# Up projections of two MLPs by Strassen's seven block products, with the residual and the hidden activations kept in DRAM

## The chip, the cores and the metric

The kernel runs on one core of a Trainium2 chip. The metric is device time in microseconds (us) of one execution. The kernel before takes 3135.95 us, the median of three runs (3134.9 to 3142.02).

## The reference

A two-layer trunk is run for two request groups that share the weights: 1024 new tokens of one stream (prompts) and 16 tokens of each of 8 running streams (samples), 1152 tokens in all, width 1024, all float32. The first layer mixes tokens by forgetting attention beside causal pooling, the second by stick-breaking attention. Behind each mixer stands an MLP, and each sub-layer is normalized, shifted and scaled by a conditioning vector, and added to the residual through a gate (w_up is 1024 x 4096, w_down 4096 x 1024):

```python
def _sq_relu_mlp(h, w_up, w_down):
    return jnp.square(jax.nn.relu(h @ w_up)) @ w_down
...
h = _rmsnorm(x, norm_g[i, 1]) * (1 + sc2) + sh2
x = x + g2 * _sq_relu_mlp(h, w_up[i], w_down[i])
```

## The kernel before

**Layout.** The residual is held transposed in SBUF, as `xT[c]`: three chunks c of 384 tokens, each with 8 blocks (`k`) of 128 channels on the partitions. Chunk 2 holds the last 256 prompt tokens and the 128 sample tokens. `h`, the normalized input, is a pair of such tiles per chunk.

**Numbers in two parts.** Every float32 operand of TensorE (PE) is a pair: a high part of type fp32r, made by a cast, and a low part, value minus high part. A product is three matmuls for each k: high by high, high by low, low by high (`lin_chunk`, L480 to L489, its matmul in L486). `split` (L181 to L187) makes the pair of a weight: the cast on ScalarE (ACT, L184), the low part on GpSimd (POOL, L185).

**An MLP.** `mlp` (L496 to L546) calls `norm` (L506), whose `norm_chunk` applies scale and shift: prompts by VectorE (DVE, L437), ACT (L440, L446), and a low part on DVE (L447) or POOL (L442); samples by L455 to L461. The sums of squares are added in L351. `up` (L509 to L524) takes one block f of 128 hidden channels, loads its weights (`load_cols`, 512 KB on the queue of SyncE, SP), and for each chunk issues 24 matmuls of 384 columns; then ACT takes the relu from PSUM (L520), DVE squares (L521), ACT casts the high part (L522) and DVE makes the low part (L523). `down` (L526 to L536) takes two such blocks, loads their rows of w_down (`load_rows`, L217), and for each chunk and each output block n issues 6 matmuls and adds the gated result to `xT` (`x_add`, L469 to L478: L472 on DVE, and for chunk 2 also L476 on DVE and L478 on POOL). The loop in L538 to L546 alternates up of one pair and down of the pair before, so hidden activations never leave SBUF.

**Order.** A scheduler orders each engine's instructions by their priority, which is the order of the code unless it is set: `at(i)` gives the norm of chunk i the priority of a place in the last down (or in the mixer's last output projection), where `pin` and `before` fix the norm's small matmuls between given output blocks (`PIN_M`, `PIN_O`). `tick` (called in up and down) issues part of the small matmuls that work out the next conditioning vectors (`ada_group`). Loads go through SP's queue, stores through ACT's.

## Time and profile before

| | |
|---|---|
| median of 3 runs | 3135.95 us (3134.9 to 3142.02) |
| the profiled execution | 3139.25 us |
| its span in the trace | 3137.4 us |
| mean granted clock of PE | 0.991 |
| busy share of the span | PE 98%, DVE 52%, ACT 33%, POOL 27% |
| moved by DMA | 330.93 MB, mean 105 GB/s |

Durations come from the one profiled execution; its time is 3.3 us above the median, and 1.85 us of it lie outside the span. An engine's busy time counts its computing instructions only. A granted clock of 1.00 is the full one. In a timeline "x3" joins three like instructions in a row, and the bracket behind a row gives the idle time ahead of it and what ended that.

### The profile page before, as it was taken

How to read it: one execution, taken by the hardware profiler on the slowest of the kernel's cores; microseconds unless marked ns; L12 is line 12 of the kernel's file. 1: busy time of each engine (PE TensorE's matmuls, PEld its weight loads, DVE VectorE, ACT ScalarE, POOL GpSimd, SP SyncE). 2: the span in 40 equal slices, each digit the busy share in tenths (PEclk: the TensorE clock that was granted, in tenths of full speed). 3: DMA queues.
4: the chain of work that ended last, by engine and by line, in shares of the span. 5: the costliest groups of instructions: out<-in, count | busy, mean ns of one | idle time of the engine just before them, and what ended most of it. 6: DMA issues, size and time to landing. Idle time of an engine off the chain costs nothing.

```text
span 3137.4 us, 51121 instructions
## 1 busy us (share of the span) xinstructions
PE 3066.5 (98%) x20558; PEld 2815.7 (90%) x20558; DVE 1637.3 (52%) x3204; ACT 1036.8 (33%) x2222; POOL 852.0 (27%) x759
## 2 busy tenths in 40 slices
PE   7999999999999999999999999999999999999998
PEld 5888868789999999999999967777789999999998
DVE  5234767674444444446300078888874444444546
ACT  5322334441212121213422276666651211212122
POOL 3212111052222222223411133443352222222222
PEclk9999999999999999999999999999999999999999
DMA  7677443312232321111555563544301111111111
GB/s 267 202 217 239 149 138 106 104 50 88 88 101 82 93 74 40 43 41 34 177 177 169 179 219 117 177 126 139 106 28 42 46 41 41 47 35 48 34 48 68
DMA packets 333617, 330.93 MB, mean 105 GB/s; under 512 B 33820, under 2 KB 292548, under 8 KB 333381
## 3 DMA queue, kind: packets, MB, share of 16 engines
q1 hardware_dynamic: 257041, 261.27, 26.9%
q10 hardware_dynamic: 76340, 66.39, 6.4%
q8 instruction: 163, 2.67, 0.4%
q14 instruction: 73, 0.60, 0.1%
HBM read 256.51 MB, written 71.09 MB: 104 GB/s over the span
## 4 chain that ended last, share of the span: by engine, by line
PE 89%; DVE 5%; DMA 2%; ACT 1%; issue 1%; POOL 1%; SPq 0%; ACTq 0%; DVEq 0%; POOLq 0%
PE ps_s L486 38%; PE ps_a L486 18%; PE ps_t L486 16%; PE ps_a L987 4%; PE ps_t L967 3%; PE ps_m L232 2%; PE ps_s L951 2%; DVE sn L905 1%; PE ps_s L952 1%; PE ps_s L1046 1%; PE ps_m L1034 1%; PE ps_t L1071 1%; DVE sg L908 1%; PE ps_s L954 1%; PE ps_t L618 0%
## 5 line engine op out<-in xcount | busy, mean ns | idle before, releaser
L185 POOL TENSOR_TENSOR w_lo<-w_raw,w_hi 128x1024 fp32r<-128x1024 f32 (+1 forms) x184 | 441.5, 2402 | 994.8 <-ACT w_hi L184 947.4
L486 PE MATMUL ps_s<-h,w_hi 128*128 128x384 f32 x2080 | 541.2, 339 | 8.1 <-DVE h L447 4.8
L184 ACT CAST w_hi<-w_raw 128x1024 fp32r<-128x1024 f32 (+1 forms) x184 | 190.4, 1049 | 935.7 <-PE ps_t L486 364.0
L472 DVE SCALAR_TENSOR_TENSOR xT<-ps_s,modT,xT 128x384 f32<-128x384 f32 (+1 forms) x516 | 294.2, 571 | 244.1 <-PE ps_s L486 242.4
L486 PEld LDWEIGHTS ps_s<-h,w_hi 128*128 128x128 f32 x2080 | 379.8, 189 | 14.9 <-DVE h L447 6.6
L478 POOL TENSOR_TENSOR xT<-xT,xs 128x128 f32<-128x128 f32 x320 | 155.8, 487 | 739.2 <-DVE xs L476 732.7
L486 PE MATMUL ps_s<-h,w_lo 128*128 128x384 f32 x1040 | 353.1, 340 | 0.0
L486 PE MATMUL ps_s<-oh,w_hi 128*128 128x384 f32 x792 | 269.1, 340 | 0.0
L486 PE MATMUL ps_s<-oh,w_lo 128*128 128x384 f32 x792 | 266.9, 337 | 0.0
L486 PE MATMUL ps_s<-ol,w_hi 128*128 128x384 f32 x792 | 266.3, 336 | 0.0
L486 PE MATMUL ps_a<-h,w_hi 128*128 128x384 f32 x944 | 244.1, 339 | 0.0
L905 DVE TENSOR_TENSOR_SCAN sn<-sn 128x128 f32<-128x128 f32 (+4 forms) x224 | 218.0, 1002 | 43.9 <-ACT sn L899 39.0
L486 PE MATMUL ps_t<-h,w_hi 128*128 128x384 f32 x816 | 210.4, 339 | 0.0
L908 POOL TENSOR_TENSOR sg<-sg,sn 128x512 f32<-128x512 f32 (+3 forms) x112 | 136.9, 1222 | 257.8 <-DVE sn L905 195.0
L523 DVE TENSOR_TENSOR ol<-r,oh 128x384 fp32r<-128x384 f32 x192 | 158.9, 829 | 86.0 <-ACT oh L522 85.5
L486 PEld LDWEIGHTS ps_s<-h,w_lo 128*128 128x128 f32 x1040 | 196.7, 189 | 0.1
L521 DVE SCALAR_TENSOR_TENSOR r<-ps_s,r 128x384 f32<-128x384 f32 x102 | 56.7, 556 | 261.2 <-ACT r L520 261.2
L472 DVE SCALAR_TENSOR_TENSOR xT<-ps_a,modT,xT 128x256 f32<-128x256 f32 (+1 forms) x252 | 143.7, 570 | 84.3 <-PE ps_a L486 83.7
L486 PEld LDWEIGHTS ps_a<-h,w_hi 128*128 128x128 f32 x944 | 171.2, 188 | 7.0 <-issue 6.7
L973 ACT COPY pt<-ps_t 128x512 f32<-128x512 f32 (+3 forms) x256 | 125.9, 498 | 128.2 <-PE ps_t L967 126.6
L486 PE MATMUL ps_s<-w_hi,h 128*128 128x256 f32 (+1 forms) x800 | 157.9, 286 | 4.4 <-ACT h L446 4.4
L486 PE MATMUL ps_a<-h,w_lo 128*128 128x384 f32 x472 | 159.8, 338 | 0.0
(306 smaller groups left out, 6849.0 us busy)
## 6 DMA issues: line engine op xcount, KB each, us to landing
w_raw<-in_w_ada_dram SPq DMA_DIRECT2D x80, 512.0 KB, 4.1
w_raw<-in_w_up_dram SPq DMA_DIRECT2D x64, 512.0 KB, 4.2
w_raw<-in_w_down_dram SPq DMA_DIRECT2D x64, 512.0 KB, 3.3
Q<-q SPq DMA_DIRECT2D x100, 256.0 KB, 3.8
q<-qt ACTq DMA_DIRECT2D x48, 384.0 KB, 5.5
vr<-in_cache_sb_v_dram SPq DMA_DIRECT2D x32, 512.0 KB, 4.9
kr<-in_cache_sb_k_dram SPq DMA_DIRECT2D x32, 512.0 KB, 4.0
out_dram<-kv ACTq DMA_DIRECT2D x48, 256.0 KB, 2.9
```

The costliest lines, as they stand in the source:

```text
L184: after(nc.scalar.copy(hi[:, :n], raw[:, :n]), "act")
L185: after(nc.gpsimd.tensor_tensor(lo[:, :n], raw[:, :n], hi[:, :n].bitcast(F32), op=ALU.subtract), "pool")
L232: nc.tensor.matmul(acc[32 * j:32 * j + 32, :], lhsT=condT[:, k, :], rhs=raws[j // 2][:, j % 2 * 512:(j % 2 + 1) * 512], start=(k == 0), st ...
L472: nc.vector.scalar_tensor_tensor(xT[c][:, n, :npc], ps[:, :npc], g[:, n, 0:1], xT[c][:, n, :npc], op0=ALU.mult, op1=ALU.add)
L478: nc.gpsimd.tensor_tensor(xT[c][:, n, 256:], xT[c][:, n, 256:], t, op=ALU.add)
L486: mm = nc.tensor.matmul(ps, lhsT=a, rhs=b, start=(i == 0), stop=(i == n - 1))
L523: nc.vector.tensor_tensor(ol[:, c], r, oh[:, c].bitcast(F32), op=ALU.subtract)
L905: nc.vector.tensor_tensor_scan(rev, rev, rev, initial=1.0, op0=ALU.mult, op1=ALU.bypass)
L908: eng.tensor_tensor(sg[:, 0:m - 1], sg[:, 0:m - 1], sn[:, 1:m], op=ALU.mult)
L967: nc.tensor.transpose(T[:, kb * P:(kb + 1) * P], pr[:, kb * P:(kb + 1) * P], ident)
L973: nc.scalar.copy(pt.rearrange("p k n -> p (k n)")[:, 0:n], T[:, 0:n])
L987: nc.tensor.matmul(A[rs, os_], lhsT=Vd[kb // 4][:, kb % 4, rs], rhs=PTs[h2][kb], start=(kb == 0), stop=(kb == i))
```

## The change

The MLP becomes two phases, `up_phase` and `down_phase`, and only up changes its arithmetic.

- **Up by seven products.** Two blocks f form a pair g, 16 pairs in all. The weights of a pair are a 2 x 2 of blocks (two halves of 512 input channels, two blocks f), and the input of a token half (`tp`, 576 of the 1152 tokens) is a 2 x 2 of blocks of 512 channels by 288 tokens. Their product takes seven block products (Strassen, in Winograd's form) in place of eight. Each is 12 matmuls of 288 columns: 4 k by three pairs of parts.
- **Forms of the input.** Seven forms of a token half (`forms`: blocks 11, 21, 22 and the sums T1 to T4) are made from the normalized input by subtractions on DVE (`sub`) and each split in two parts (`parts`): the cast on ACT, the low part on POOL for two in three and on DVE for the third. The norm is applied in place, in `X`, which is now one tile.
- **Forms of the weights.** For each pair four loads of 256 KB (`raw_block`) and four sums on DVE, and each of seven forms is split by `w_parts`, on ACT and POOL.
- **Putting together.** Products are added in PSUM where they can be, and with DVE where not (`add`, `finish`); P2's square is taken from PSUM. Freed columns of `X` serve as scratch (`slot`).
- **Passes.** Pairs 0 to 2 are done on the first token half alone, then pairs 0 to 2 on the second, then 3 to 14 on both with one set of weights, then 15 on the second and on the first. `late` spreads the norm of the rest and the forms of the second half over the first three passes.
- **DRAM.** The residual is stored chunk by chunk behind the mixer's last output projection (on SP) and read back in `down_phase`; hidden activations are stored by up (on ACT's queue, 144 KB each) and read back in rows of 1152 tokens, and split there.
- **Down** takes four blocks f at a time (12 matmuls between two `x_add` calls), the first time with the chunks in the order 2, 1, 0.

The core of the diff; its last lines are those of the mixer's output projection.

```diff
-A1 = 0.25
+A1 = 0.3
...
-PIN_M = (4, 11)
+PIN_M = (2, 6)
+TB = 288
+UR = 6
+UW = 4
+UG = 3
+DR = 4
+HB = 6
...
-    xT = [const.tile([P, KD, CW], F32, name=f"xT{c}") for c in range(NCH)]
+    X = const.tile([P, KD, T_ALL], F32, name="xT")
+    xT = [X[:, :, c * CW:(c + 1) * CW] for c in range(NCH)]
+    x_sc = [dram.tile([P, KD, CW], F32, name=f"x{c}") for c in range(NCH)]
+    hid_sc = [dram.tile([2, P, T_ALL], F32, name=f"hid{g}") for g in range(FF // P // 2)]
...
+    def up_phase(l):
...
+        w = w_up[l]
+        forms = ("11", "21", "T2", "T1", "T3", "22", "T4")
...
+            def apply(c, sd, k, c0, c1):
+                x = xT[c][:, k, c0:c1]
+                nc.vector.scalar_tensor_tensor(x, x, A[:, k, 0:1], sd[:, c0:c1], op0=ALU.mult, op1=ALU.mult)
+                nc.scalar.activation(x, x, AF.Identity, bias=B[:, k, 0:1])
...
+            def parts(form, tp, j, src):
+                hi, lo = (t[:, j, :] for t in F[form][tp])
+                rr["f"] = rr.get("f", 0) + 1
+                nc.scalar.copy(hi, src)
+                (nc.vector if rr["f"] % 3 == 0 else nc.gpsimd).tensor_tensor(lo, src, hi.bitcast(F32), op=ALU.subtract)
...
+            def sub(o, a, b):
+                nc.vector.tensor_tensor(o, a, b, op=ALU.subtract)
+            def other_forms(tp, j):
+                b11, b12, b21, b22 = (blk(tp, j, r, c) for r in (1, 2) for c in (1, 2))
+                parts("22", tp, j, b22)
+                sub(b11, b12, b11)
+                sub(b12, b22, b12)
+                sub(b22, b22, b11)
+                parts("T2", tp, j, b22)
+                parts("T1", tp, j, b11)
+                parts("T3", tp, j, b12)
+                sub(b21, b21, b22)
+                parts("T4", tp, j, b21)
...
+            KO = (0, 4, 1, 5, 2, 6, 3, 7)
+            with at(0):
+                sd = rstd_of(0, np_, 0)
+                for i, k in enumerate(KO):
+                    apply(0, sd, k, 0, TB)
+                    if i % 2:
+                        first_forms(0, i // 2)
+                for k in KO:
+                    apply(0, sd, k, TB, CW)
+            with at(1):
+                sd1 = rstd_of(1, np_, 1)
+                h1 = 2 * TB - CW
+                for i, k in enumerate(KO):
+                    apply(1, sd1, k, 0, h1)
+                    if i % 2:
+                        other_forms(0, i // 2)
+            pins.clear()
+            def late():
...
+                for k in KO:
+                    apply(1, sd1, k, h1, CW)
+                yield
+                sd = rstd_of(2, np_, 2)
+                yield
+                for i, k in enumerate(KO):
+                    apply(2, sd, k, 0, 256)
+                    if i % 2 == 0:
+                        samples(sd, i // 2 * 2, i // 2 * 2 + 2)
+                    if i % 2:
+                        yield
+                for j in range(4):
+                    first_forms(1, j)
+                    yield
+                for j in range(4):
+                    other_forms(1, j)
+                    yield
...
+            def raw_block(g, r, c):
+                t = ur.tile([P, 4, P], F32, name="u_raw", tag="raw", bufs=UR)
+                f = 2 * g + r - 1
+                nc.sync.dma_start(t, w[(c - 1) * 512:c * 512, f * P:(f + 1) * P].rearrange("(k p) n -> p k n", p=P))
...
+            def w_parts(src):
+                hi = uw.tile([P, 4, P], F32R, name="u_hi", tag="hi")
+                lo = uw.tile([P, 4, P], F32R, name="u_lo", tag="lo")
+                nc.scalar.copy(hi, src)
+                nc.gpsimd.tensor_tensor(lo, src, hi.bitcast(F32), op=ALU.subtract)
+                return hi, lo
...
+                def form(self, f):
+                    a = self.a
+                    if f == "P6":
+                        sub(a[2, 1], a[1, 1], a[2, 1])
+                        s2 = ur.tile([P, 4, P], F32, name="u_raw", tag="raw", bufs=UR)
+                        sub(s2, a[2, 2], a[2, 1])
+                        a["s2"] = s2
+                        return w_parts(s2)
+                    if f == "P5":
+                        nc.vector.tensor_tensor(a[1, 1], a["s2"], a[1, 1], op=ALU.add)
+                    if f == "P3":
+                        sub(a[1, 2], a[1, 2], a["s2"])
+                    return w_parts(a[{"P1": (1, 1), "P2": (1, 2), "P5": (1, 1), "P7": (2, 1), "P3": (1, 2), "P4": (2, 2)}[f]])
...
+            FORM = {"P1": "11", "P2": "21", "P6": "T2", "P5": "T1", "P7": "T3", "P3": "22", "P4": "T4"}
...
+            def product(p, ws, tp, ps, start):
+                wh, wl = ws
+                mh, ml = F[FORM[p]][tp]
+                i = 0
+                for k in range(4):
+                    for a, b in ((wh, mh), (wh, ml), (wl, mh)):
+                        mm = nc.tensor.matmul(ps, lhsT=a[:, k, :], rhs=b[:, k, :], start=(start and i == 0), stop=(i == 11), skip_group_check=not start)
...
+            def out(u, r, c, t):
+                tok = (2 * u["tp"] + c - 1) * TB
+                nc.scalar.dma_start(hid_sc[u["g"]][r - 1, :, tok:tok + TB], t)
...
+            def add(o, ps, b):
+                nc.vector.tensor_tensor(o, ps, b, op=ALU.add)
...
+            def finish(u, r, c, ps, b):
+                t = slot("h", 8, 8)
+                add(t, ps, b)
+                nc.vector.scalar_tensor_tensor(t, t, 0.0, t, op0=ALU.max, op1=ALU.mult)
+                out(u, r, c, t)
...
+                    if p == "P1":
+                        u["b1"] = ps_t()[:, :TB]
+                        product(p, ws, tp, u["b1"], True)
+                        u["p1"] = slot("p1", 0, 4)
+                        nc.scalar.copy(u["p1"], u["b1"])
+                    elif p == "P2":
+                        product(p, ws, tp, u["b1"], False)
+                        t = slot("h", 8, 8)
+                        nc.scalar.activation(t, u["b1"], AF.Relu)
+                        nc.vector.scalar_tensor_tensor(t, u["b1"], 0.0, t, op0=ALU.max, op1=ALU.mult)
+                        out(u, 1, 1, t)
+                    elif p == "P6":
+                        u["b2"] = ps_s()[:, :TB]
+                        product(p, ws, tp, u["b2"], True)
+                        u["u2"] = slot("u2", 4, 2)
+                        add(u["u2"], u["b2"], u["p1"])
+                    elif p == "P5":
+                        u["b3"] = (ps_a if tp else ps_s)()[:, :TB]
+                        product(p, ws, tp, u["b3"], True)
+                        u["p15"] = slot("p15", 6, 2)
+                        add(u["p15"], u["b3"], u["p1"])
+                    elif p == "P7":
+                        product(p, ws, tp, u["b2"], False)
+                        finish(u, 2, 2, u["b2"], u["p15"])
+                    elif p == "P3":
+                        product(p, ws, tp, u["b3"], False)
+                        finish(u, 1, 2, u["b3"], u["u2"])
+                    elif p == "P4":
+                        product(p, ws, tp, u["b2"], False)
+                        finish(u, 2, 1, u["b2"], u["p1"])
...
+            NG = FF // P // 2
+            passes = ([(g, (0,)) for g in range(UG)] + [(g, (1,)) for g in range(UG)]
+                      + [(g, (0, 1)) for g in range(UG, NG - 1)] + [(NG - 1, (1,)), (NG - 1, (0,))])
+            fill = late()
+            prev = None
+            for i, (g, tps) in enumerate(passes):
+                if i == UG:
+                    for _ in fill:
+                        pass
+                us, wts = [{"g": g, "tp": tp} for tp in tps], Weights(g)
+                for p in ("P1", "P4", "P2", "P6", "P5", "P7", "P3"):
+                    if p == "P4":
+                        if prev:
+                            stage(p, *prev)
+                    else:
+                        stage(p, us, wts)
+                    next(fill, None)
+                prev = us, wts
+            stage("P4", *prev)
+    def down_phase(l):
...
+            for c in (2, 1, 0):
+                for k in range(KD):
+                    nc.sync.dma_start(xT[c][:, k, :], x_sc[c][:, k, :])
+            NF = FF // P
+            for f0 in range(0, NF, DR):
+                last = f0 + DR == NF
+                if last and l == 0:
+                    have((1, 2))
                 ws, hs = [], []
...
+                for f in range(f0, f0 + DR):
+                    raw = hid.tile([P, NCH, CW], F32, name="hr", tag="hr", bufs=3)
+                    nc.sync.dma_start(raw.rearrange("p c n -> p (c n)"), hid_sc[f // 2][f % 2])
+                    ws.append(load_rows(w_down[l], f * P, wx if f % 2 else None))
+                    oh, ol = (hid.tile([P, NCH, CW], F32R, name=n, tag=n, bufs=HB) for n in ("oh", "ol"))
+                    nc.scalar.copy(oh, raw)
+                    nc.vector.tensor_tensor(ol, raw, oh.bitcast(F32), op=ALU.subtract)
+                    hs.append((oh, ol))
+                if last:
+                    order = [(c, n) for c in range(NCH) for n in range(KD)]
+                elif f0 == 0:
+                    order = [(c, n) for c in (2, 1, 0) for n in range(KD)]
+                else:
+                    order = [(c, n) for n in range(KD) for c in range(NCH)]
                 for c, n in order:
...
                         if last:
                             pin(c, n, mm, PIN_O)
+                            nc.sync.dma_start(x_sc[c][:, n, :], xT[c][:, n, :])
...
```

Three excerpts of the order of instructions follow. Line numbers in the second fence of each are those of the changed kernel.

First, POOL at the start of the MLP of layer 1, before: low parts of weights (L185), of the normalized chunks (L442), and the samples.

```order
L185 TENSOR_TENSOR w_lo<-w_raw,w_hi 128x1024
L478 TENSOR_TENSOR xT_74<-xT_74,xs 128x128
L442 TENSOR_TENSOR h_24206<-xa,h_24205 128x384
L351 TENSOR_TENSOR sb<-sb,nw 128x384
L442 TENSOR_TENSOR h_24206<-xa,h_24205 128x384 x3
L185 TENSOR_TENSOR w_lo<-w_raw,w_hi 128x1024
L442 TENSOR_TENSOR h_24208<-xa,h_24207 128x384 x4
```

POOL at the same place now: low parts of the forms of the first token half (L548, tiles F and FT) and of the first weight forms (L622).

```order
L548 TENSOR_TENSOR F_25027<-xT,F_25026 128x288 x2
L622 TENSOR_TENSOR u_lo<-u_raw,u_hi 128x512 x3
L548 TENSOR_TENSOR FT_25019<-xT,FT_25018 128x288
L548 TENSOR_TENSOR F_25027<-xT,F_25026 128x288
L548 TENSOR_TENSOR FT_25019<-xT,FT_25018 128x288
L548 TENSOR_TENSOR FT_25023<-xT,FT_25022 128x288 x2
L548 TENSOR_TENSOR FT_25015<-xT,FT_25014 128x288
L548 TENSOR_TENSOR FT_25019<-xT,FT_25018 128x288
L548 TENSOR_TENSOR FT_25023<-xT,FT_25022 128x288
L622 TENSOR_TENSOR u_lo<-u_raw,u_hi 128x512
```

Where 8 low parts of two chunks stood among two of weights, 19 low parts of the first half now stand among the weights' low parts, and as many of the second half follow.

Second, SP at the start of the MLP of layer 1, before: loads of w_up and w_down alone.

```order
L217 DMA w_raw<-in_w_down_dram 128x1024
L195 DMA w_raw<-in_w_up_dram 128x8x128 x2
L217 DMA w_raw<-in_w_down_dram 128x1024 x2
L195 DMA w_raw<-in_w_up_dram 128x8x128 x2
L217 DMA w_raw<-in_w_down_dram 128x1024 x2
```

SP now: loads of weight blocks (L615), and among them the reloads of chunk 2 of the residual (L746) into columns that the forms of the second half are made from.

```order
L615 DMA u_raw<-in_w_up_dram 128x4x128 x8
L746 DMA xT<-x_72 128x384
L615 DMA u_raw<-in_w_up_dram 128x4x128 x2
L746 DMA xT<-x_72 128x384 x2
L615 DMA u_raw<-in_w_up_dram 128x4x128
L746 DMA xT<-x_72 128x384 x4
L615 DMA u_raw<-in_w_up_dram 128x4x128
L746 DMA xT<-x_72 128x384
L615 DMA u_raw<-in_w_up_dram 128x4x128 x63
```

The eight reloads of chunk 2 came in ahead of the weights of the fourth pass; a reload waits for the last reader of its columns.

Third, ACT where the first operands of down are made in layer 0, before: casts of hidden activations (L522) stand right behind each relu (L520), among the norm's.

```order
L520 ACTIVATE r<-ps_s 128x384
L440 ACTIVATE xa<-xa,modT 128x256
L520 ACTIVATE r<-ps_s 128x384
L446 ACTIVATE h_7007<-xa,modT 128x256
L441 CAST h_7007<-xa 128x256
L522 CAST oh<-r 128x384
L460 CAST h_7007<-xs 128x3x128
L522 CAST oh<-r 128x384
```

ACT now, at the end of up: the last stores of hidden activations (L669), casts of w_down (L202), and the casts of the rows read back (L758).

```order
L669 DMA hid_88<-xT 128x288
L202 CAST w_hi<-w_raw 128x1024
L669 DMA hid_88<-xT 128x288
L758 CAST oh<-hr 128x1152 x3
L202 CAST w_hi<-w_raw 128x1024 x2
L758 CAST oh<-hr 128x1152 x3
L202 CAST w_hi<-w_raw 128x1024
```

Down's casts moved behind the last store of up, and take whole rows of 1152 tokens.

## Rows read from the trace of the kernel before

**Rows 1.** The page's first part: busy time, share of the span, instructions.
```profile
PE 3066.5 (98%) x20558; PEld 2815.7 (90%) x20558; DVE 1637.3 (52%) x3204; ACT 1036.8 (33%) x2222; POOL 852.0 (27%) x759
```

**Rows 2.** By stretch: from:to, us, busy PE, PEld, DVE, ACT, POOL, PEclk, DMA share, GB/s.
```profile
642.00:1490.00 848.00, 845.12 (x4846) 818.73 (x4847) 409.94 (x785) 192.33 (x331) 239.16 (x219) 1.00 0.22 68
2302.00:3123.00 821.00, 817.10 (x4674) 816.21 (x4673) 405.81 (x777) 187.50 (x321) 235.64 (x219) 1.00 0.14 42
```

**Rows 3.** The chain in order of time, in up of layer 1: start, us, link.
```profile
2373.37 4.22 PE ps_s L486 x24
2377.59 4.21 PE ps_t L486 x24
```

**Rows 4.** PE's timeline at the second mixer: start, us; the second is 24 matmuls later.
```profile
1590.35 0.28 PE L486 MATMUL ps_s<-w_hi,h 128*128 128x256 f32 x1
...
1593.17 0.28 PE L486 MATMUL ps_a<-w_hi,h 128*128 128x256 f32 x1
```

**Rows 5.** PE's timeline at the MLP start of layer 1, first, third and last of it.
```profile
2303.83 0.62 PE L486 MATMUL ps_s<-h,w_hi 128*128 128x384 f32 x2 [1.67 <-ACT h L446]
...
2306.69 0.69 PE L486 MATMUL ps_s<-h,w_hi 128*128 128x384 f32 x1 [2.23 <-DVE h L447]
...
2311.01 0.52 PE L486 MATMUL ps_s<-h,w_hi 128*128 128x384 f32 x1
```

**Rows 6.** By stretch: the MLP start of layer 1, and the busiest DMA.
```profile
2300.00:2310.00 10.00, 6.09 (x28) 5.58 (x28) 9.85 (x18) 5.85 (x12) 7.80 (x7) 0.74 0.17 53
1540.00:1560.00 20.00, 19.34 (x165) 19.14 (x164) 1.12 (x2) 3.91 (x11) 0.89 (x1) 1.00 0.83 264
```

**Rows 7.** POOL's timeline: two places where DVE waits beside it.
```profile
641.52 2.36 POOL L185 TENSOR_TENSOR w_lo<-w_raw,w_hi 128x1024 fp32r<-128x1024 f32 x1
...
2341.35 4.79 POOL L185 TENSOR_TENSOR w_lo<-w_raw,w_hi 128x1024 fp32r<-128x1024 f32 x2 [4.74 <-ACT w_hi L184]
```

**Rows 8.** DVE's timeline at the same places, and the MLP start of layer 1.
```profile
642.14 2.15 DVE L351 TENSOR_TENSOR sa<-sa,nw 128x384 f32<-128x384 f32 x1
...
2301.60 1.65 DVE L437 SCALAR_TENSOR_TENSOR xa<-xT,Ad,ps_a 128x384 f32<-128x384 f32 x3
...
2343.96 3.53 DVE L523 TENSOR_TENSOR ol<-r,oh 128x384 fp32r<-128x384 f32 x3
```

**Rows 9.** By line: ns of one at least, median, most; first to last start.
```profile
L523 DVE TENSOR_TENSOR ol<-r,oh x192: 545/559/2593, 660.0 to 3094.0; 128x384 fp32r<-128x384 f32 x192
...
L521 DVE SCALAR_TENSOR_TENSOR r<-ps_s,r x102: 543/558/560, 658.0 to 3092.9; 128x384 f32<-128x384 f32 x102
...
L437 DVE SCALAR_TENSOR_TENSOR xa<-xT,Ad,ps_a x96: 468/603/616, 43.0 to 2334.2; 128x384 f32<-128x384 f32 x64, 128x256 f32<-128x256 f32 x32
...
L442 POOL TENSOR_TENSOR h<-xa,h x48: 733/1017/1384, 45.8 to 2335.9; 128x384 fp32r<-128x384 f32 x32, 128x256 fp32r<-128x256 f32 x16
...
L773 POOL TENSOR_TENSOR pw<-w_raw,pw x1: 1290/1290/1290, 88.3 to 88.3; 128x512 fp32r<-128x512 f32 x1
...
L772 ACT CAST pw<-w_raw x1: 616/616/616, 85.8 to 85.8; 128x512 fp32r<-128x512 f32 x1
...
L459 POOL TENSOR_TENSOR xs<-xs,modT x12: 620/846/906, 75.4 to 2334.1; 128x384 f32<-128x384 f32 x8, 128x256 f32<-128x256 f32 x4
...
L659 ACTq DMA_DIRECT2D q<-qt x36: 520/521/906, 88.3 to 1813.2; - x36
```

**Rows 10.** DMA issues: KB each, median us from issue to landing.
```profile
w_raw<-in_w_up_dram SPq DMA_DIRECT2D x64, 512.0 KB, 4.2
w_raw<-in_w_down_dram SPq DMA_DIRECT2D x64, 512.0 KB, 3.3
```

More of the change, by code (lines that the diff above doesn't have):

```diff
@@ new lines, in up_phase @@
+            ur = es.enter_context(tc.tile_pool(name=f"ur{l}", bufs=1, side="right", reuse_waits="tile"))
+            uf = [es.enter_context(tc.tile_pool(name=f"uf{l}{tp}", bufs=1, reuse_waits="tile",
+                                                **({"side": "right"} if tp == 0 else {}))) for tp in range(2)]
+            uw = es.enter_context(tc.tile_pool(name=f"uw{l}", bufs=UW, side="right", reuse_waits="tile"))
+            F = {f: [[uf[tp].tile([P, 4, TB], F32R, name=f"F{f}{i}", tag=f"F{f}{i}") for i in range(2)] for tp in range(2)]
+                 for f in forms}
@@ new lines, in up_phase, with slot @@
+            FORM = {"P1": "11", "P2": "21", "P6": "T2", "P5": "T1", "P7": "T3", "P3": "22", "P4": "T4"}
+            last = {}
+            cnt = {}
+            def slot(kind, base, n):
+                i = cnt[kind] = cnt.get(kind, -1) + 1
+                i = base + i % n
+                return X[:, i % KD, i // KD * TB:(i // KD + 1) * TB]
+            def product(p, ws, tp, ps, start):
[5 more added lines that the diff above has]
+                        mm = nc.tensor.matmul(ps, lhsT=a[:, k, :], rhs=b[:, k, :], start=(start and i == 0), stop=(i == 11), skip_group_check=not start)
+                        if i == 0 and "mm" in last:
+                            behind(mm, last["mm"])
+                        i += 1
+                last["mm"] = mm
@@ L532, in down, with mlp, __init__ @@
                                    for (wh, wl), (oh, ol) in zip(ws, hs)])
-                    x_add(c, n, ps, g, mp)
-                    tick(0.25)
+                    x_add(c, n, ps, g, hid)
+                    tick(0.5)
                     if last:
                         pin(c, n, mm, PIN_M)
-            prev = (0, up(0, 1, order=M_ORD))
-            for f in range(2, FF // P, 2):
-                cur = up(f)
-                down(*prev, False)
-                cur += up(f + 1)
-                prev = (f, cur)
-            if l == 0:
-                have((1, 2))
-            down(*prev, True)
+    def mlp(l):
+        close_weights()
+        up_phase(l)
+        open_weights(f"wpool{l + 1}")
+        down_phase(l)
     class Npool:
         B = {"sa": 1, "sb": 1, "nw": 2, "xa": 3, "rc": 2}
-        def __init__(self, pool):
-            self.pool = pool
+        def __init__(self, pool, bufs=None):
+            self.pool, self.B = pool, bufs or self.B
         def tile(self, shape, dt, name, tag):
```

92 lines of the change are left out of this document (51 added, 41 removed).

## Prediction

> **What bounds the kernel now.** I read the page's first part, then a table by stage, then the timelines of single engines. TensorE (PE) is busy 98% of the span [rows 1], and in the two MLPs it is the only bound: 845.1 of 848 us and 817.1 of 821 us, at a granted clock of 1.00 [rows 2]. VectorE (DVE) and GpSimd (POOL) are busy about half and a quarter of the time there. So an MLP is worth its matmuls, and only PE columns saved, or PE made to wait, can move the end.
>
> A 384-column matmul starts every 4.215 / 24 = 175.6 ns [rows 3], and 24 matmuls of 256 columns take 2.82 us, 117.5 ns each [rows 4]. Both are 0.458 ns a column.
>
> The one weak place is the start of each MLP. PE idles 1.67 and 2.23 us, and the 13 matmuls behind that come 0.32 us apart, the 1.2 GHz level, granted clock 0.74 in that slice [rows 5, 6]. It loses 3.9 + 13 x (0.332 - 0.176) = 5.9 us in all, while ScalarE (ACT), DVE and POOL normalize and split the activations.
>
> The rows to remember are those of DVE beside POOL. A DVE operation whose two tensors both lie in SBUF stands still while a POOL operation runs: 0.55 us of work took 2.15 beside a POOL operation of 2.36, three took 3.53 behind the second of two, and they ended 1.35 us after it, 0.45 each [rows 7, 8]. L523 (two SBUF tensors) reads 545 at best and 2593 ns at worst; L521 and L437 (one of them in PSUM) never move [rows 9]. POOL waits for DVE in the same way: L442 goes from 1017 to 1384 ns [rows 9].
>
> **The gain.** Before, up is 32 x 3 x 24 = 2304 matmuls of 384 columns in a layer: 404.6 us. After, 16 pairs of f, two token halves, seven products of 12: 2688 of 288 columns. No row has 288; the bounds are 117.5 and 175.6 ns. I take 132.0, on the line between, since both ends have the same price per column; an end would need a step in it, so I keep 3% of doubt. 2688 x 132.0 = 354.8 us, **49.8 saved in a layer, 99.6 in both**. The Trainium skill (TensorE: Matmul & The Clock Gate, Back-to-back issue gap) gives N / 2.4 GHz + 2.5 ns, an estimate of 162.5 and 122.5 ns here, and 45.1 saved in a layer. The trace disagrees with its 162.5, so the rows stand; by the page the sum would be 9 us higher.
>
> Down has as many matmuls of the same width, at nothing. Its x_add calls halve, on a DVE that does not bound. The ada matmuls only change place.
>
> **What replaces it at the start.** Seven forms of each activation block, and of each weight block, must be made and split, and most of this is DVE work on two SBUF tensors or POOL work. By the rows above those two do not overlap, so I add them up. Prices [rows 9]: POOL 512 columns 1.29 us, 288 columns 0.80 (between 0.733 at 256 and 1.017 at 384), 384 columns 1.0; DVE, from the 0.45 at 384, 0.34 at 288 and 0.60 at 512.
>
> - Forms of one token half: 28 low parts, two thirds on POOL (19 x 0.80) and 9 x 0.34 on DVE, and 16 subtractions x 0.34: 23.7 us. Twice.
> - Norm of the third chunk: 3 x 1.0 + 4 x 0.45, and 8 POOL operations for the samples, at 0.62 (L459's least): 9.8.
> - Weights of the three passes ahead of the second half: 20 low parts x 1.29, 12 subtractions x 0.60, 8 finishes x 0.34: 35.7. In layer 0 four of each of the first two stand ahead of the start by the order: 28.1.
>
> Together 92.9 us in layer 1 and 85.3 in layer 0. In front stand 32 apply operations on DVE, 11.5 us by L437, beside which POOL finds about 4 us of work: 7.5 more. So the second half's forms are ready at T + 93 (layer 0) and T + 100 (layer 1), T being where DVE begins to apply the norm (2301.6 in layer 1, [rows 8]). Three passes on that half follow, each with 7 x 1.29 + 4 x 0.60 + 3 x 0.34 = 12.4 us of this work for 84 x 0.132 = 11.1 of PE: T + 130 and T + 137. PE has 6 x 11.1 = 66.5 us of work by then. It **loses 63.5 and 70.5 us, 57.6 and 64.6 more than now**. Passes on both halves need 13.4 us for 22.2 of PE, so from there PE bounds again.
>
> That rule is in the Trainium skill too (SBUF — State Buffer, Who interferes with whom): an exclusive lock for a whole instruction, for DVE with two SBUF inputs against a GpSimd read. The rows agree at 384 and 1024 columns; for 288 no run here shows it. Without it the sum is that of the first rival.
>
> ACT is no bound: a single pass costs it 7 x 0.62, two PSUM reads of about 0.5 and four store issues of 0.52 [rows 9], 7.4 us. Nor is DMA: 1.05 MB of weights and 0.59 MB of stores in 11.1 us are 148 GB/s, where 264 are seen [rows 6]; a mean of 100 in the other passes.
>
> **Three smaller waits**, each per layer. On SP four weight loads of the fourth pass stand behind reloads of x that wait for the second half's forms; a load lands in 4.2 us [rows 10], and two products of 1.6 us lie ahead: 0 to 6, I take 2. The last two passes are single again (12.4 for 11.1), with four weight buffers ahead: 0 to 3, take 1. Between up and down, the first hidden rows are read behind reloads that wait for the last stores, and ACT's splits of them stand behind the last store issue. One landing of about 4 us [rows 10] and an ACT and a DVE pass over 1152 columns: 3 to 13, take 6, as the weights are split by then.
>
> **Sum.** Layer 0: 57.6 + 9 - 49.8 = +16.8. Layer 1: 64.6 + 9 - 49.8 = +23.8. The profiled execution took 3139.25 us, so 3179.9; the median of the runs is 3.3 below it, so **3177 us**.
>
> **Rivals.** *Faster: the two engines overlap well enough that POOL alone sets the start.* Many of DVE's operations here are only 0.34 us and may slip in where POOL waits for ACT. POOL's own work is 38 x 0.80 + 8.0 + 16 (layer 1: 20) x 1.29 = 59 and 64 us, with the 7.5 in front T + 67 and T + 72; the next three passes run at PE's 11.1. PE loses 33.5 and 38.5, 27.6 and 32.6 more than now, plus 5 each: 33 + 38 - 100 = -29, so 3107. For it speaks that DVE has other work to do beside POOL; against it the rows, where even one operation waited POOL out. It decides from about 48 us lost at the start.
>
> *Slower still: the chain through PSUM.* P7, P3 and P4 add into a bank that DVE must read first, and that read is queued on DVE behind operations that wait for POOL. A POOL operation (1.29) for each of 18 such products in six single passes is 23 us a layer: 3223. In double passes another product lies between, so it is hidden there. PE at 1.2 GHz after each gap would add to it.
>
> *The change doesn't do what it says* is not open: the order has the 288-column matmuls in these numbers. Only their price is, at 10 us a layer.
>
> **How the numbers follow.** Forecast 0.55 (its own range 3125 to 3220), first rival 0.28, second 0.12, the rest (price of 288, the turn to down at 13 us) 0.05. About 0.3%, 9 us, is what a measurement can tell from no change. Faster: the first rival but for its slow end, and a little of the rest, 0.30; same 0.08; slower 0.62. Below 3095 and above 3230 I leave 0.1 each.
>
> **What would show it.** Right: 288-column products 1.58 us apart in the middle; 60 to 70 us of PE idle in the first 130 us of each MLP, ended by POOL's low parts or DVE's subtractions; L548 and L559 on DVE well over 0.4 us in the mean; then PE full; up about 418 us a layer; some 6 us idle ahead of down. Wrong: matmuls of 288 columns off 132 ns, DVE's subtractions at 0.4 us beside a busy POOL, idle below 48 us at the start, or PE waiting in the double passes.

## The result, and the profile after

The changed kernel takes 3236.56 us (median of four runs, 3232.93 to 3239.55), the kernel before 3135.54: ratio 1.0318, interval 1.0305 to 1.0331, some 101 us slower. The forecast was 3177, slower by 41, with a range up to 3230. The direction was right, the size was less than half of it.

The profiled execution after takes 3239.55 us, its span 3237.4, 100.0 us longer than before. The page's first part after, which answers to [rows 1]:

```profile
PE 3030.2 (94%) x21326; PEld 2762.5 (85%) x21326; DVE 1748.0 (54%) x3213; ACT 1107.4 (34%) x2360; POOL 1133.7 (35%) x902
```

PE has less to do and idles more; POOL does 282 us more. To see where, I cut both traces at the same work. Before, PE's timeline at the last of the norm's small matmuls (L372) and the last matmul of down, in both layers:

```profile
639.81 0.83 PE L372 MATMUL ps_a<-cst,rc 128*128 128x128 f32 x6
...
1487.51 0.34 PE L486 MATMUL ps_t<-oh,w_lo 128*128 128x384 f32 x1
...
2301.33 0.83 PE L372 MATMUL ps_a<-cst,rc 128*128 128x128 f32 x6
...
3121.12 0.34 PE L486 MATMUL ps_t<-oh,w_lo 128*128 128x384 f32 x1
```

After, the same places, and between them the last matmul of up and the first of down (the bracket is the idle time ahead and what ended it):

```profile
646.11 0.83 PE L391 MATMUL ps_a<-cst,rc 128*128 128x128 f32 x6
...
1075.53 0.29 PE L661 MATMUL ps_s<-FT,u_lo 128*128 128x288 f32 x1
...
1086.70 0.69 PE L505 MATMUL ps_a<-oh,w_hi 128*128 128x384 f32 x1 [2.97 <-ACT oh L758]
...
1541.56 0.34 PE L505 MATMUL ps_t<-oh,w_lo 128*128 128x384 f32 x1
...
2364.12 0.83 PE L391 MATMUL ps_a<-cst,rc 128*128 128x128 f32 x6
...
2794.54 0.45 PE L661 MATMUL ps_s<-FT,u_lo 128*128 128x288 f32 x1
...
2800.36 0.69 PE L505 MATMUL ps_a<-oh,w_hi 128*128 128x384 f32 x1 [5.37 <-ACT oh L758]
...
3224.17 0.34 PE L505 MATMUL ps_t<-oh,w_lo 128*128 128x384 f32 x1
```

The differences of these starts give the first MLP 847.7 us before and 895.5 after (+47.8), the second 819.8 and 860.1 (+40.3). The rest of the 100 is in the first mixer (+6.3), the second (+8.7) and the end (-3.1). A part of this is work that only changed its place: the first MLP holds 192 of the conditioning matmuls (29.7 us of PE) where it held 176 (24.5), and the first mixer 16 fewer (42.7 us for 47.3).

The forecast had +16.8 and +23.8 for the MLPs, so with before's 847.7 and 819.8 it expected 864.5 and 843.6. Part by part:

| | forecast, layer 0 | measured | forecast, layer 1 | measured |
|---|---|---|---|---|
| up, with the wait ahead | 421.3 | 429.4 | 428.3 | 430.4 |
| turn from up to down | 6 | 11.2 | 6 | 5.8 |
| down (what is left of the sum) | 437.2 | 454.9 | 409.3 | 423.8 |
| both mixers and the end | 0 | 12.0 together | | |

By stage (from:to, us, busy us and instructions of PE, PEld, DVE, ACT, POOL, PEclk, DMA share, GB/s), the two ups, the two downs and a piece of the middle of up:

```profile
646.10:1075.70 429.60, 379.13 (x2707) 373.95 (x2706) 255.94 (x464) 145.27 (x304) 239.46 (x188) 0.93 0.33 102
1086.70:1541.70 455.00, 446.11 (x2524) 416.97 (x2524) 197.23 (x322) 79.00 (x90) 127.23 (x101) 0.98 0.37 130
2364.10:2794.70 430.60, 375.12 (x2708) 369.50 (x2706) 268.09 (x468) 147.23 (x308) 249.89 (x191) 0.95 0.33 103
2800.40:3224.30 423.90, 417.27 (x2364) 414.65 (x2365) 205.12 (x317) 74.10 (x84) 131.12 (x99) 0.99 0.25 87
...
800.00:850.00 50.00, 50.00 (x377) 50.00 (x376) 22.70 (x48) 13.46 (x26) 21.95 (x16) 1.00 0.32 101
```

In the middle 377 matmuls take 50 us, 132.6 ns each, and PE is full: the price of 288 columns and the double passes came out as forecast. Before, PE idled for 3 to 4 us in a whole MLP [rows 2]; now the two downs alone idle 8.9 and 6.6 us, at a granted clock below 1.00.

### The profile page after: what moved, and what is told of

It is laid out like the page before. It is cut to its first block, busy times and chain, and to the rows that moved or that the text cites. A ratio compares the mean times of both kernels' runs of the same rounds, so it can differ in the third digit from the quotient of the medians.

```text
span 3237.4 us, 54634 instructions
## 1 busy us (share of the span) xinstructions
PE 3030.2 (94%) x21326; PEld 2762.5 (85%) x21326; DVE 1748.0 (54%) x3213; ACT 1107.4 (34%) x2360; POOL 1133.7 (35%) x902
## 4 chain that ended last, share of the span: by engine, by line
PE 66%; DVE 5%; DMA 2%; issue 1%; POOL 1%; ACT 1%; SPq 0%; DVEq 0%; POOLq 0%; ACTq 0%
PE ps_s L505 20%; PE ps_s L661 11%; PE ps_a L505 9%; PE ps_t L505 8%; PE ps_t L661 5%; PE ps_a L661 3%; PE ps_a L1221 2%; PE ps_t L1201 2%; DVE sn L1139 1%; PE ps_s L1185 1%; PE ps_s L1280 1%; PE ps_s L1186 1%; DVE xT L559 1%; PE ps_m L1268 1%; DMA hr<-hid 1%
## 5 line engine op out<-in xcount | busy, mean ns | idle before, releaser
L622 POOL TENSOR_TENSOR u_lo<-u_raw,u_hi 128x512 fp32r<-128x512 f32 x280 | 395.6, 1417 | 350.8 <-ACT u_hi L621 345.0
L661 PE MATMUL ps_s<-FT,u_hi 128*128 128x288 f32 x1792 | 372.6, 301 | 32.1 <-DVE xT L672 24.2
L202 ACT CAST w_hi<-w_raw 128x1024 fp32r<-128x1024 f32 (+1 forms) x120 | 125.4, 1049 | 603.4 <-PE ps_s L505 504.8
L661 PEld LDWEIGHTS ps_s<-FT,u_hi 128*128 128x128 f32 x1792 | 295.6, 193 | 35.7 <-ACT u_hi L621 15.9
L621 ACT CAST u_hi<-u_raw 128x512 fp32r<-128x512 f32 x280 | 172.3, 619 | 405.6 <-PE ps_s L661 194.7
L661 PE MATMUL ps_s<-FT,u_lo 128*128 128x288 f32 x896 | 269.9, 301 | 9.4 <-POOL u_lo L622 9.3
L661 PE MATMUL ps_t<-F,u_hi 128*128 128x288 f32 x1024 | 216.2, 305 | 50.3 <-ACT xT L688 30.7
L672 DVE TENSOR_TENSOR xT<-ps_s,xT 128x288 f32<-128x288 f32 x256 | 116.5, 456 | 224.7 <-PE ps_s L661 222.8
L661 PEld LDWEIGHTS ps_t<-F,u_hi 128*128 128x128 f32 x1024 | 170.8, 195 | 53.5 <-ACT xT L688 32.9
L661 PEld LDWEIGHTS ps_s<-FT,u_lo 128*128 128x128 f32 x896 | 172.7, 193 | 10.8 <-POOL u_lo L622 10.8
L505 PEld LDWEIGHTS ps_s<-oh,w_hi 128*128 128x128 f32 x816 | 156.7, 192 | 13.4 <-issue 7.2
L759 DVE TENSOR_TENSOR ol<-hr,oh 128x1152 fp32r<-128x1152 f32 x64 | 140.1, 2222 | 46.9 <-ACT oh L758 46.7
```

Of the source, the lines that this page charges most:

```text
L202: after(nc.scalar.copy(hi[:, :n], raw[:, :n]), "act")
L505: mm = nc.tensor.matmul(ps, lhsT=a, rhs=b, start=(i == 0), stop=(i == n - 1))
L621: nc.scalar.copy(hi, src)
L622: nc.gpsimd.tensor_tensor(lo, src, hi.bitcast(F32), op=ALU.subtract)
L661: mm = nc.tensor.matmul(ps, lhsT=a[:, k, :], rhs=b[:, k, :], start=(start and i == 0), stop=(i == 11), skip_group_check=not start)
L672: nc.vector.tensor_tensor(o, ps, b, op=ALU.add)
```

## The experiments

All times are medians; the ratio is against the kernel before on the same chip, which took 3136.4 to 3138.6 us beside these runs and 3135.5 beside the changed kernel, so differences of up to 3 us between runs are not read. Each edit starts from the changed kernel unless it says otherwise.

**The start of up.** The forecast's reason was that DVE operations on two SBUF tensors and POOL operations exclude each other, so that their sum counts. The trace after shows it. DVE, then POOL, at 660 us:

```profile
661.09 7.34 DVE L559 TENSOR_TENSOR xT<-xT 128x288 f32<-128x288 f32 x7
...
663.43 6.61 POOL L548 TENSOR_TENSOR FT<-xT,FT 128x288 fp32r<-128x288 f32 x7 [0.15 <-ACT FT L547]
```

Seven subtractions of 288 columns take 7.34 us, 1.05 each, beside low parts that take 0.79 us at the least (L548); one of them stands beside a low part of 512 columns, which lengthens it. On POOL's side a low part together with a subtraction takes 0.94 us, seven in 6.61. By line (ns at least, median, most), first after, then in `e2_all_dve`, the run below that has no low parts of up on POOL:

```profile
L559 DVE TENSOR_TENSOR xT<-xT x64: 443/1042/1548, 658.1 to 2453.8; 128x288 f32<-128x288 f32 x64
```

```profile
L559 DVE TENSOR_TENSOR xT<-xT x64: 444/452/475, 659.9 to 2421.3; 128x288 f32<-128x288 f32 x64
```

The same 64 subtractions: median 1042 ns beside POOL, 452 without it.

`e1_wlo_dve`, the weights' low parts to DVE:

```diff
 def w_parts(src):
-    nc.gpsimd.tensor_tensor(lo, src, hi.bitcast(F32), op=ALU.subtract)
+    nc.vector.tensor_tensor(lo, src, hi.bitcast(F32), op=ALU.subtract)
```

> The changed kernel with the weights' low parts (L622) moved from POOL to DVE. Lock theory (DVE operations on two SBUF tensors and POOL operations exclude each other, and their sum sets the start of up): some 42 low parts of the six single passes cost 0.6 in place of 1.29 us, 29 us a layer less, so about 3237 - 58 = 3180 us, with the waits at the start of up down from about 55 to about 30 us a layer. POOL theory (POOL's own work sets the start): POOL sheds 42 x 1.29 = 54 us a layer, nearly all of the loss: about 3130. A chain through ACT's order of casts alone: within 10 us of 3237. In all cases the waits in down and at the ends of the mixers stay as they are.

Measured 3211.9 us (ratio 1.0235, 1.022 to 1.0251), 25 less than the changed kernel. POOL's pace alone is out: it would have given 3130. The lock theory's saving was twice too large.

`e3_flo_dve`, the input's low parts to DVE:

```diff
-(nc.vector if rr["f"] % 3 == 0 else nc.gpsimd).tensor_tensor(lo, src, hi.bitcast(F32), op=ALU.subtract)
+nc.vector.tensor_tensor(lo, src, hi.bitcast(F32), op=ALU.subtract)
```

> The changed kernel with all low parts of the input's forms (L548) on DVE, the weights' left on POOL. Lock theory: 38 POOL operations of 0.80 us a layer become DVE operations of 0.25 to 0.37, 16 to 21 us a layer less: 3237 - 37 = 3200 us. POOL theory: 38 x 0.80 = 30 us a layer less, 3176. A chain through ACT's order alone: within 10 us of 3237.

Measured 3220.0 (1.026, 1.0245 to 1.0276), 17 less: again less than half of the 37.

`e2_all_dve`, both edits at once:

> The changed kernel with all low parts of up, the weights' and the input's, on DVE. Lock theory: POOL drops out of the start, so nothing excludes DVE any more; the two single moves gave 25 and 17 us, and together they give their sum or more: 3195 or less. If DVE by itself is then what sets the start (it was busy 17 to 20 us of each 20 there): less than the sum, some 30 us, about 3207, with DVE full in the first 100 us of up. POOL theory: POOL is out of the way, so the start loses nothing but its first 10 us: about 3130.

Measured 3204.67 (1.0216, 1.0201 to 1.0232), 32 less, not the sum of 41. It is the case in which DVE itself sets the start. Its trace by stretch, columns as above:

```profile
646.00:700.00 54.00, 33.44 (x193) 30.22 (x191) 52.85 (x139) 39.75 (x105) 13.78 (x14) 0.78 0.16 53
700.00:730.00 30.00, 22.43 (x130) 21.34 (x131) 29.99 (x69) 13.53 (x29) 0.00 (x0) 0.77 0.49 145
```

DVE is busy 82.8 of these 84 us, with POOL nearly empty, and PE still idles: DVE is full. Its timeline there gives the price of its operations with POOL out of the way, from start to start 0.60 us for 512 columns and 0.37 for 288:

```profile
665.43 0.68 DVE L622 TENSOR_TENSOR u_lo<-u_raw,u_hi 128x512 fp32r<-128x512 f32 x1
666.03 0.45 DVE L548 TENSOR_TENSOR FT<-xT,FT 128x288 fp32r<-128x288 f32 x1
666.40 0.45 DVE L559 TENSOR_TENSOR xT<-xT 128x288 f32<-128x288 f32 x1
```

Why did the moves give half? The expectations had charged DVE's own time already, so that is not the reason. They took a low part on POOL and a DVE operation beside it as the sum of both, some 1.16 us. The pair takes 0.94, and two operations on DVE take 0.74, so the move of one low part of the input gives 0.2 us and not 0.43 or more. As an estimate, 38 of them in two layers make 15 us, where 17 were measured. For the weights no such account was tried, and why only 25 of the 58 us came stays open.

`e10_hybrid` asks whether it is the amount of work or the chain of the first forms. It starts from `e9_combo` (below) and does the first four pairs, on each token half, with the four plain blocks, of which the parts of block 12 borrow T4's tiles:

```diff
-            passes = ([(g, (0,)) for g in range(UG)] + [(g, (1,)) for g in range(UG)]
-                      + [(g, (0, 1)) for g in range(UG, NG - 1)] + [(NG - 1, (1,)), (NG - 1, (0,))])
+            PLAIN = (None, ("11", "T4"), ("21", "22"))
...
+                for r, c in order:
...
+                    for h in (1, 2):
+                        mh, ml = F[PLAIN[h][c - 1]][tp]
+                        wh, wl = ws[r, h]
+                        for k in range(4):
+                            for a, b in ((wh, mh), (wh, ml), (wl, mh)):
+                                mm = nc.tensor.matmul(ps, lhsT=a[:, k, :], rhs=b[:, k, :], start=(i == 0), stop=(i == 23))
...
+            passes = [(g, (0, 1)) for g in range(NC, NG - 1)] + [(NG - 1, (1,)), (NG - 1, (0,))]
...
+            for g in range(NC):
+                plain(g, 0, fill, CM if g == 0 else RM)
...
+            for g in range(NC):
+                plain(g, 1, fill, ((1, 2), (2, 2), (1, 1), (2, 1)) if g == NC - 1 else CM if g == 0 else RM)
```

> The kernel of the last line, and the first four pairs computed on each token half with the four plain blocks (eight products of 12 matmuls, 1.6 us of PE more for a pass) in place of the seven forms: the seven products begin with the passes on both halves. A plain pass wants 4 low parts of weights and 4 squares on DVE (some 4 us for 12.7 of PE) where a single pass of seven products wants some 10 for 11.1. If the loss at the start is the amount of DVE and POOL work per PE time, DVE has some 89 us to do in PE's first 102, and the start loses some 10 us and pays 8 x 1.6 = 13, against 43 in the run with all low parts on DVE: 20 us a layer less, 3188 - 40 = 3148. If it is the chain of the first forms (norm, cast, low part) and not the amount, the plain passes only add their 26 us: about 3200.

Measured 3151.27 (1.0045, 1.003 to 1.006), 42 less than `e9_combo`, some 32 of them in the two ups by the traces. The amount of work per PE time, as forecast, gives that number. By stretch:

```profile
646.00:700.00 54.00, 43.81 (x270) 42.15 (x271) 48.68 (x129) 38.63 (x108) 14.05 (x12) 0.81 0.20 61
700.00:800.00 100.00, 100.00 (x753) 100.00 (x752) 57.29 (x117) 35.16 (x75) 0.00 (x0) 1.00 0.46 139
```

From 700 us on PE is full, as the changed kernel is only from 780 on:

```profile
760.00:780.00 20.00, 16.82 (x124) 16.29 (x123) 12.98 (x20) 6.41 (x12) 14.13 (x11) 1.00 0.41 121
780.00:800.00 20.00, 20.00 (x152) 20.00 (x152) 10.08 (x22) 5.66 (x11) 9.55 (x7) 1.00 0.34 106
```

The plain passes take PE 8/7 of the time of single passes of seven products, which is 26 us in all, and the loss falls by more than twice that. The norm, the casts and the low parts of the first forms are still there, so that chain alone is refuted. But a plain pass also leaves out P1's copy and the sums read from PSUM, so the run does not part the amount of work from the chain through PSUM; no run here does.

Two attempts to win more from this failed. `e12_start` sets ACT's order at the start by hand:

```diff
-                nc.scalar.activation(x, x, AF.Identity, bias=B[:, k, 0:1])
+                i = nc.scalar.activation(x, x, AF.Identity, bias=B[:, k, 0:1])
+                if "cast" in late_after:
+                    behind(i, late_after["cast"])
...
+                for h in (1, 2):
+                    pre[1, h] = w_parts(raw0[1, h])
```

> The kernel with plain first passes, and ACT's order at the start set by hand: the first forms' casts ahead of the rest of the norm, the first weights' casts at the front. In layer 1 PE waits 14 us there for a weight cast that stands behind 29 applications of the norm on ACT (10 us); if that order is the cause, 6 to 9 us less there, about 3144 us in all; if the weights or DVE are late in any case, no change, 3151.

Measured 3158.58 (1.0068, 1.0054 to 1.0082), not faster: in layer 1 PE now waits 10.0 us ahead of up in place of 14.3, but 7.4 in place of 1.6 behind that, and in layer 0 the wait for the norm's sums of the third chunk grows from 4.7 to 8.7.

`e12_nc3`, the same with `NC = 3` for 4:

> The same with three plain pairs in place of four: 2 x 1.6 us of PE less in each layer. If DVE has done its forms by then (it waits for nothing behind the first 30 us in the run with four), 6 us less than that kernel, about 3138; if the amount of DVE work decides again, with 26 us of PE less to cover it, the same time or some us more.

Measured 3151.85 (1.0047, 1.0034 to 1.0059): some 7 us less than `e12_start`, as expected of PE's shorter work, and level with `e10_hybrid`. No kernel here beats the one before.

**Down and the turn.** `e7_classic` separates the phases and keeps the old up:

```diff
+            norm(l, 1, hh, hl, Npool(np_), M_ORD)
...
+                        lin_chunk(ps, [((wh[:, k], wl[:, k]), (hh[c][:, k, :], hl[c][:, k, :])) for k in range(KD)])
...
+                        nc.vector.scalar_tensor_tensor(r, ps, 0.0, r, op0=ALU.max, op1=ALU.mult)
+                        nc.scalar.dma_start(hid_sc[f // 2][f % 2, :, c * CW:(c + 1) * CW], r)
...
-                    nc.sync.dma_start(xT[c][:, k, :], x_sc[c][:, k, :])
...
-                            nc.sync.dma_start(x_sc[c][:, n, :], xT[c][:, n, :])
```

> The two phases and the hidden activations through DRAM, but up as before (24 matmuls of 384 columns on the normalized chunks), and the residual kept in SBUF: the separation alone, without the seven products. If down loses time because it reads and splits hidden rows in groups of four (31 us in both layers by the trace) and at the turn (17 us): 3136 + 48 = 3184 us. If those losses belong to the seven products' reloads and their half-clock stretches: 3136 + 12 = 3148, the turn alone. The changed kernel against this one is then the net worth of the seven products.

Measured 3184.63 (1.0152, 1.0137 to 1.0167): the separation alone costs 46 us, and the seven products, forecast to win 99.6 of PE's time, cost another 52. The forecast had 12 for the separation, the two turns, and 29 for the seven products with their starts. So the separation carries some 34 of the 60 us that it fell short, and the seven products the rest. PE's timeline at its turn and at the last group of down, layer 1:

```profile
2747.07 0.69 PE L505 MATMUL ps_a<-oh,w_hi 128*128 128x384 f32 x1 [9.51 <-ACT oh L559]
...
3107.54 0.45 PE L505 MATMUL ps_s<-ol,w_hi 128*128 128x384 f32 x1 [1.88 <-DVE ol L560]
...
3111.27 0.69 PE L505 MATMUL ps_s<-oh,w_lo 128*128 128x384 f32 x1 [1.51 <-POOL w_lo L203]
```

Its two downs take 445.8 and 421.0 us, 8.6 and 11.7 above what the forecast had for down, the first with 24 conditioning matmuls fewer than the forecast's down had. The last group stalls in the changed kernel too. There, in layer 0, PE and then SP's queue:

```profile
1481.20 0.45 PE L505 MATMUL ps_s<-oh,w_lo 128*128 128x384 f32 x1 [2.21 <-POOL w_lo L203]
...
1483.52 0.69 PE L505 MATMUL ps_s<-oh,w_lo 128*128 128x384 f32 x1 [1.52 <-POOL w_lo L203]
```

```profile
1441.51 16.74 SPq L247 DMA_DIRECT2D araw<-in_w_ada_dram  x4
1458.30 23.20 SPq L235 DMA_DIRECT2D w_raw<-in_w_down_dram  x4
```

The last group takes its output blocks in a fixed order and wants four pairs of weights at once. SP issues their loads over 23 us, behind four loads for the conditioning matmuls that it issues over 17.

`e5_dr2` takes groups of two:

```diff
-DR = 4
+DR = 2
...
-tick(0.5)
+tick(0.25)
```

> The changed kernel with down in groups of two blocks f, as before, in place of four (six pairs of hidden rows in the buffers, so four ahead and not two). If the extra time in down comes from a group of four that finds only two of its weight and row pairs ready where the order of the output blocks is fixed (the last group: 5.8 us of waits for w_lo and ol, and half the clock behind them): 12 to 20 us less, about 3221. If it comes from splitting whole rows again on DVE beside POOL, which is the same work in either grouping: within 4 us of 3237. DVE then adds twice as many blocks to the residual, which hides behind PE as it did before.

Measured 3228.06 (1.0293, 1.0275 to 1.031), 8.5 less. PE's waits for the last group's weights and rows are gone from its trace in layer 0. Down takes 446.9 and 414.9 us in place of 454.9 and 423.8, so 17 less in its trace, whose execution (3220.03) was the fastest of its four. The group of four is a part of the loss; 9.7 and 5.6 us over the forecast stay.

`e6_ada`, the conditioning matmuls sooner:

```diff
-A1 = 0.3
+A1 = 0.45
```

> The changed kernel with the conditioning matmuls of layer 0's down taken faster (A1 0.45 in place of 0.3), so that their loads on SP are through before the loads of the last group's weights. If SP's queue is what makes the last group's four w_lo late in layer 0 (5.8 us of waits and about 5 us of half clock behind them): 6 to 11 us less, about 3228. If POOL's 2.4 us for each of the four is what makes them late: no change, 3237.

Measured 3225.62 (1.0288, 1.0273 to 1.0303), 11 less. Its down of layer 0 takes 448.3, 6.6 less, and layer 1 is nearly unchanged (422.6). PE idles 5.2 us in it in place of 8.9, and the four waits for w_lo (5.8 us) have become one of 1.5, with 2.6 for `ol`: SP's queue made the weights late, but it is not the whole of the last group's wait. In its trace the first mixer ended 4.8 us sooner with nothing edited in it, so not all of the 11 is the edit's.

`e9_combo` is `e2_all_dve`, `e5_dr2` and `e6_ada` together:

> Three changes at once: all low parts of up on DVE (alone 32 us less), down in groups of two (8.5 less), and the conditioning matmuls of layer 0's down taken faster (11 less, some of it perhaps in the first mixer, where nothing was changed). If the three act in different places, as their traces say, they add up: 3237 - 32 - 8.5 - 6 to 11 = 3185 to 3190 us. If they mend the same loss: about 3205.

Measured 3193.28 (1.0178, 1.0161 to 1.0195): 43 less, where the three alone gave 32, 8.5 and 11. That is 8 short of the sum. The low parts of up and the rest do add: its ups take 406.2 and 414.4 us, as with `e2_all_dve` (404.8 and 414.3). The other two do not: down of layer 0 takes 446.1, where `e5_dr2` alone had 446.9 and `e6_ada` alone 448.3. Both mend the same wait of the last group.

**The mixers.** PE waits 5.9 us in each for the norm's sums (L371 on DVE), where it waited 0 and 3.1 us before. `e4_x_act`:

```diff
-nc.sync.dma_start(x_sc[c][:, n, :], xT[c][:, n, :])
+nc.scalar.dma_start(x_sc[c][:, n, :], xT[c][:, n, :])
```

> The changed kernel with the 24 stores of the residual in each mixer's last output projection issued on ACT's queue in place of SP's. If the new waits there (PE 5.9 us for the norm's sums, twice) come from SP, where the first weight blocks queue behind stores that wait for the output projection, and DVE then stands on such a block: 5 to 12 us less, about 3228. If DVE's own load (the weights' sums) is what delays the norm: within 3 us of 3237, or slower by some us, as ACT has 24 more issues of 0.3 to 0.5 us.

Measured 3235.61 (1.0314, 1.0297 to 1.0331): no change. SP's queue is not the cause.

`e8_hold`, where `held["n"]` is the first application of the norm on DVE:

```diff
-                        sub(a[2, 1], a[1, 1], a[2, 1])
+                        i = nc.vector.tensor_tensor(a[2, 1], a[1, 1], a[2, 1], op=ALU.subtract)
+                        if self.g == 0:
+                            behind(i, held["n"])
```

> The changed kernel with the first pair's weight sums on DVE (L559 and what hangs on them) held behind the first application of the norm. If DVE's in-order wait for weight blocks, and these sums, delay the norm's own sums in the mixer's last output projection (PE waits 5.9 us there in each layer): 6 to 12 us less at the end of the mixers, of which up to 4 come back as later weights: about 3230. If the norm's sums wait for ACT or POOL: within 3 us of 3237.

Measured 3234.69 (1.0316, 1.03 to 1.0331): no change in all. In its trace the first mixer ends 6.7 us sooner, but the wait for the norm's sums fell only from 5.9 to 3.9 there and to 5.6 in the second. The first up then takes 7 us more: the weight sums stand among the forms on DVE now (651 to 661 us), and PE waits 6.1 us there for a low part on DVE in place of 1.9, and 26.5 for P1's copy in place of 22.9.

## Why the prediction was wrong

**The gain** held: 132.6 ns measured for 132.0, and 377 matmuls in each 50 us.

**The start of up** held in its sum, not in its parts. From the starts above, up takes 429.4 and 430.4 us; less 2688 x 0.133 = 357.5, PE loses 71.9 and 72.9, forecast 66.5 and 73.5 with the two small waits. Idle time is only 50.5 and 55.5 of it (the table by stage), the rest slow matmuls; in the first 130 us PE idles 47.3 and 51.5, where the prediction wanted 60 to 70 and called less than 48 a sign against itself. The forms of the second half were ready at T + 83 and T + 93 (the last low parts on POOL end at 728.3 and 2456.1 us, T is 645.6 and 2363.6), where the sum said 93 and 100. It charged 0.34 us for each DVE operation, and beside POOL those of 288 columns add some 0.15 (0.94 for a pair, less POOL's 0.79); over the 50 of them that is an estimate of 9.5 us, where the sum missed by 10 and 7. But PE did not begin on the second half then. Its first product there starts at 739.96 and 2456.31 us, T + 94 and T + 93: in layer 0 the first three passes, with their own waits, held PE for 12 us after the forms were ready, so there the sum's step, PE waiting for the second half's forms, was not what bound. One thing that the sum left out is PE's clock. After a wait of 14.8 us the products run at the 1.2 GHz level (the granted clock is 0.50 from 660 to 680 us). PE's timeline after, each low-part matmul one third of a group; the last two rows are the first matmuls on the second half:

```profile
671.73 0.85 PE L661 MATMUL ps_t<-F,u_hi 128*128 128x288 f32 x2 [14.83 <-ACT xT L688]
672.38 0.44 PE L661 MATMUL ps_t<-F,u_lo 128*128 128x288 f32 x1
672.62 0.68 PE L661 MATMUL ps_t<-F,u_hi 128*128 128x288 f32 x2
673.10 0.44 PE L661 MATMUL ps_t<-F,u_lo 128*128 128x288 f32 x1
...
739.96 0.68 PE L661 MATMUL ps_t<-F,u_hi 128*128 128x288 f32 x2
...
2456.31 0.43 PE L661 MATMUL ps_t<-F,u_hi 128*128 128x288 f32 x2
```

Three matmuls from 672.38 to 673.10, 0.240 us each in place of 0.133. Some 115 of them ran so in the first start and 80 in the second: 12 and 8 us. I had this as one sentence under a rival. That the misses nearly cancelled is luck.

**The rivals.** POOL alone is refuted by `e1_wlo_dve` and by the rows of L559. The chain through PSUM is there: in the first start 36 us of PE's waits end with P1's copy on ACT (L688) or with the reads of L672 on DVE (total, count, longest):

```profile
PE ps_t L661 <- ACT xT L688: 22.9, 3, 14.8
PE ps_s L661 <- DVE xT L672: 13.5, 5, 6.4
```

The rival had the reads alone; P1's copy nobody priced. It waits in ACT's order behind casts that themselves wait for DVE's subtractions, as ACT's timeline ahead of PE's wait of 14.83 us shows:

```profile
670.40 0.43 ACT L547 CAST FT<-xT 128x288 fp32r<-128x288 f32 x1 [1.50 <-DVE xT L559]
...
671.29 0.38 ACT L688 COPY xT<-ps_t 128x288 f32<-128x288 f32 x1
```

I take the chain for the form in which the lack of DVE and POOL time shows, as up came within 9 us of the sum without it. This is argued: the sum was off in other terms too, and no run takes the chain out by itself.

**The step that failed** is "Down has as many matmuls of the same width, at nothing". It was over by 17.7 and 14.5 us, the largest miss. I counted its matmuls, saw DVE far from its bound, and asked only what happens at the turn. What the runs showed in its place: a wait where the last group of four is issued in fixed order (5.8 us in layer 0, 4.4 in layer 1), short waits elsewhere, mostly for the first groups (3.1 and 2.2), the half clock behind them (40 and 29 matmuls at 0.320 in place of 0.175: 5.8 and 4.2 us), and in layer 0 1.9 us of conditioning matmuls that the first mixer held before. That leaves 1.1 and 3.7 us open. In layer 0 SP's queue ahead of the last group has a share in this: with it freed, down gives back 6.6 us, though 4.1 us of waits at the last group stay (`e6_ada`). `e7_classic` has 20 of the 32 us without a single product of the seven.

**Not counted at all** were the mixers, 15 us before what the end gives back, and 5 us at the first turn, where a load for the conditioning matmuls stood between (4.5 us of PE's wait, and 3.4 for eight of these matmuls). In the second mixer 4.0 us of it is the next norm's first activation, late behind the end of down. The wait for the norm's sums is new in the first (5.9) and grew from 3.1 to 5.9 in the second; in `e8_hold` the work taken out of there came back behind it. The first mixer's end moved between 641 and 648 us in runs that left it as it was, so its 6.3 us cannot be put down to the change with certainty. What delays the sums there stays open.

By size, of the 60 us between 3179.9 forecast for the profiled execution and 3239.55: down 32, the mixers and the end 12, up 10, the turn 5.

## What to carry to other kernels

When a phase is cut in two, price the second half as carefully as the half that changes: its first and last groups, what each queue has to issue ahead of them, and the clock behind each wait. Work for DVE and POOL that excludes itself is paid nearly as a sum (0.94 us for a pair of 0.79 and 0.37), so take it off the stretch where PE has little cover (here by plain products first, 42 us) rather than move it between the two. And ask of a saving on PE how much other work it makes per microsecond of PE: the seven products save 47 us of PE in a layer (2304 x 0.1756 less 2688 x 0.133), and wanted 83 us of a full DVE first (`e2_all_dve`).

## What the runs showed of the hardware

- DVE and POOL exclude each other for most of an operation, not for the whole of it as the prediction reckoned. A DVE subtraction of 288 columns takes 0.37 us in a row of its own, but adds only some 0.15 to POOL's 0.79 when the two alternate (0.94 for both).
- A DVE operation with one operand in PSUM is not held: L672 reads 441 at least, 458 in the median and 460 ns at most over 256 calls, those beside the start's POOL work among them. The Trainium skill (SBUF — State Buffer, Who interferes with whom) has a DVE instruction with at most one SBUF input, outside its two-port modes, free of GpSimd; the rows agree.
- Half clock costs 0.107 us on a 288-column matmul and 0.145 on one of 384, and in the two ups and downs some 260 matmuls paid it.
